# One quarter of u moved inside its own tile, so that 12 of every 84 products read both sides at one place

## The chip, the cores and the metric

The kernel runs on one core of one Trainium2 chip. The metric is the device time of one execution in microseconds (us), the median of several. A core has a matrix engine (TensorE, "PE" in the profile; its weight loads are shown as a row of their own, "PEld"), a vector engine (VectorE, "DVE"), an activation engine (ScalarE, "ACT"), a general engine (GpSimd, "POOL") and a queue engine that issues DMAs (SyncE, "SP").

## The reference

Two layers are computed on a sequence of 512 tokens with 1024 features: a gated recurrent mixer in the first, a dilated attention in the second, and a SwiGLU feed-forward part behind each. The change touches the feed-forward part alone:

```python
def swiglu_ffn(u, w_in, w_out):          # u: 512 x 1024, w_in: 1024 x 5632, w_out: 2816 x 1024
    gate, up = jnp.split(u @ w_in, 2, axis=-1)
    return (jax.nn.silu(gate) * up) @ w_out
```

All of it is float32. The kernel gets there by splitting each operand into a rounded part and a remainder (`hi`, `lo`; type fp32r) and adding three products.

## The kernel before, in words

`u` lies transposed in two tiles, `uh` (the rounded part) and `ul` (the remainder): 128 partitions, 8 slices of features (`kt`), 512 tokens each. Every product of the matrix engine is one of a group of three, issued by `three` on lines 438 to 440: line 438 multiplies hi by hi, line 439 takes the remainder of the side that streams, line 440 the remainder of the weights. In the feed-forward part the weights are loaded into the array (128 columns) and `u` streams through it.

The first few column blocks of `w_in` go by plain products, 512 tokens wide (`block`; 24 products a block). The other 34 blocks, 16 in the first layer and 18 in the second, go by Strassen's scheme in Winograd's form (`seven_products`): a block of 1024 by 256 columns (128 of the gate, 128 of up) is cut into quarters, and so is `u`; seven products of quarters take the place of eight. One product of quarters is one call of `run`: 4 slices of `kt` times `three`, so 12 products on PE, each 256 tokens wide. A block is 7 calls of `run`, 84 products.

The quarters of `u` are slices of `uh` and `ul`: `B11` is slices 0 to 3, tokens 0 to 255; `B21` is slices 4 to 7 of the same tokens; `B22` is slices 4 to 7 of tokens 256 to 511. The fourth quarter, slices 0 to 3 of tokens 256 to 511, isn't a side of a product; it only goes into the sums of quarters. These sums (`t1`, `T3`, `T4`, `t2`) are made once a layer by `token_sums` and lie in tiles of their own, `th` and `tl`. The weights of a block are prepared by DVE, ACT and POOL while PE works on the block before: ACT casts (`r_hi`, line 797; `s_hi`, line 821), DVE subtracts (`r_lo`, line 801; `s_lo`, line 825), and POOL and DVE form sums of quarters (`sum_a` on POOL, line 805; `sum_b`, `sum_c` on DVE, lines 809 and 813). They lie in two sets of tiles in turn, `R` (called `spare` or `hiq`/`loq` in the trace) and `Sm`. The results are put together in `shared` (`sums_1`, `sums_2`, `sums_3`, `finish`, and ACT's copies on lines 884 and 894).

The order of the work inside `seven_products` is written out by hand (`manual_schedule`); what stands ahead of that block is put in order by a scheduler when the program is built.

A word on "place". Each tile begins at a fixed byte of its partition, and place here means that byte modulo 512. In the program as built, `uh` begins at 28288, `ul` at 44672, `th` at 147072 and `tl` at 163456, all at place 128. The weights of `R` and `Sm` begin at 134336, 140480 or 82112, for example, all at place 192, because of an offset of 16 elements (`R0`). In the plain products both sides are at place 128. In the attention layer's `seven_values` the sides are exchanged: slices of `u` and its sums are loaded as weights, at place 128, and the matrix streams, at place 256 (`V0`). Slices of 256 or 512 tokens and of 128 columns are multiples of 512 bytes long, so a tile's place holds for all of its slices.

Of the kernel before, what the change touches and what calls it, by code (L numbers as in the profile page):

```python
# [9 lines left out]
F32 = mybir.dt.float32  # L10
# [148 lines left out]
def block_kernel(tc, x, c, positions, ada_w, ada_b, norm_g, hgrn_w_in, lower, hgrn_norm_g, hgrn_w_out,  # L159
                 attn_w_in, attn_w_out, ffn_w_in, ffn_w_out, inv_freq, out):  # L160
    nc = tc.nc
    act, dve, pool, pe = nc.scalar, nc.vector, nc.gpsimd, nc.tensor
# [5 lines left out]
    with ExitStack() as ctx:  # L168
# [7 lines left out]
        def bank(tag):  # L176
            uid[0] += 1
            return psum.tile([P, 512], F32, name=f"ps_{tag}{uid[0]}", tag=tag, bufs={"mm": 4, "a": 2, "b": 2}[tag])

        def fresh(p, shape, tag, bufs=1, dt=F32):  # L180
            uid[0] += 1
            return p.tile(shape, dt, name=f"{tag}{uid[0]}", tag=tag, bufs=bufs)
# [247 lines left out]
        uh = base.tile([P, KT, S], F32R, name="uh")  # L430
        ul = base.tile([P, KT, S], F32R, name="ul")
# [5 lines left out]
        def three(ps, ah, al, bh, bl, start, stop):  # L437
            pe.matmul(ps, ah, bh, start=start, stop=False)  # L438
            pe.matmul(ps, ah, bl, start=False, stop=False)  # L439
            pe.matmul(ps, al, bh, start=False, stop=stop)  # L440
# [18 lines left out]
        class Turn:  # L459
# [61 lines left out]
            def u_of(self, t, q, ks=range(4)):  # L521
                if ks[0] == 0:
                    self.u[t, q] = fresh(self.pl, [P, 4, P], "u", 4)
                u, b = self.u[t, q], self.b[t][q]
                for k in ks:
                    kt = q * 4 + k
                    A, B, src = self.A[:, kt:kt + 1], self.B[:, kt:kt + 1], b[:, k * P:(k + 1) * P]
                    if q == 0:
                        act.activation(u[:, k], src, AF.Identity, bias=B, scale=A)
                    else:  # L530
                        dve.tensor_scalar(u[:, k], src, A, B, op0=OP.mult, op1=OP.add)
# [239 lines left out]
        def seven_products(fs, mid, sgp, spare, th, tl):  # L771
# [4 lines left out]
            Q4 = lambda a: a.rearrange("p (s n) -> p s n", s=4)  # L776
            u_of = lambda r, c: [(uh[:, r * 4 + k, c * 256:c * 256 + 256], ul[:, r * 4 + k, c * 256:c * 256 + 256]) for k in range(4)]
            t_of = lambda i: [(th[:, i, k], tl[:, i, k]) for k in range(4)]
            B11, B21, B22 = u_of(0, 0), u_of(1, 0), u_of(1, 1)
            t1, T3, T4, t2 = (t_of(i) for i in range(4))  # L780

            W = shared.rearrange("p a (b n) -> p (a b) n", b=2)
# [4 lines left out]
            def places(i):  # L787

                p = i % 2
                if len(ring) <= p:  # L790
                    ring.append((spare if p == 0 else st.part_tiles(R0), st.part_tiles(R0)))
                return ring[p]
# [37 lines left out]
            def run(ps, w, o, us):  # L830
                for kt in range(4):
                    a = slice(o + kt * P, o + (kt + 1) * P)
                    three(ps, w[0][:, a], w[1][:, a], *us[kt], kt == 0, kt == 3)

            def runs(i):
                R, Sm = places(i)
                b = [bank("mm") for _ in range(4)] if i % 2 == 0 else [bank(t) for t in "abab"]
                g_of[i] = b
                half = lambda n, k: b[n][:, k * 256:k * 256 + 256]
                run(half(0, 0), R, 0, B11)  # L840
                run(half(3, 1), R, 512, T4)
                run(half(1, 0), R, 1024, B21)
                run(half(1, 1), Sm, 0, t2)
                run(half(2, 1), Sm, 1024, T3)
                run(half(2, 0), Sm, 512, t1)
                run(half(3, 0), Sm, 1536, B22)
# [20 lines left out]
            with tc.manual_schedule(engines=ORDERED):  # L867
# [9 lines left out]
                for i in range(len(fs)):  # L877
                    more = i + 1 < len(fs)
                    runs(i)
                    sums_3(i - 1)  # L880
                    if more:
                        r_lo(i + 1)
                    finish(i - 1)
                    act.copy(W[:, 2], g_of[i][0][:, 0:256])
                    if more:
                        sum_a(i + 1)
                        sum_b(i + 1)
                        s_hi(i + 1, 0)
                        sum_c(i + 1)
                    sums_1(i)  # L890
                    if more:
                        s_lo(i + 1, 0)
                        s_hi(i + 1, 1)
                    act.copy(W[:, 3], g_of[i][2][:, 0:256])
                    if more:
                        s_lo(i + 1, 1)
                        r_hi(i + 2)
                    sums_2(i)
# [3 lines left out]
        def ffn(l, first, close, nxt, side):  # L902
            turns.close()
            close()
            with ExitStack() as fx:
# [4 lines left out]
                with ExitStack() as qx:  # L910
                    sgp = qx.enter_context(tc.tile_pool(name=f"sg{l}", bufs=1, side=side))
                    qp = qx.enter_context(tc.tile_pool(name=f"quarters{l}", bufs=1, side=bass.opposite_side(side)))
                    spare = [qp.tile([P, 3 * 512 + R0 - k * R0], F32R, name=f"spare{l}{k}")[:, R0 - k * R0:] for k in range(2)]
                    qp.tile([P, 112], F32, name=f"pad_q{l}")
                    th = qp.tile([P, 4, 4, 256], F32R, name=f"th{l}")
                    tl = qp.tile([P, 4, 4, 256], F32R, name=f"tl{l}")
                    for j in range(PLAIN[l]):
                        if j == 0:
                            pss = first
                        else:  # L920
                            pss = []
                            for i in range(2):
                                w = st.take()
                                pss += [block(*w, k * P, 256) for k in range(2)]
                        sg = [fresh(sgp, [P, S], "sg", 2) for _ in range(2)]
                        for k in range(2):
                            act.activation(sg[k], pss[k], AF.Silu)
                        if j == 0:
                            cut = token_sums(th, tl, midt[:, NF - 8:])
                        for k in range(2):  # L930
                            dve.tensor_mul(mid(2 * j + k), pss[2 + k], sg[k])
                        if j == 0:
                            cut()
                            fixed.close()
                    seven_products(range(2 * PLAIN[l], NF), mid, sgp, spare, th, tl)
# [136 lines left out]
        first, vraw, vhi, vlo = {}, {}, {}, {}  # L1072
# [538 lines left out]
        first = mixer_out(oT, otp, (8,), gates.pop((0, 2)), 0, "left", lambda: None)  # L1611
# [263 lines left out]
        first = mixer_out(oT, store[0], (3, 5), gates.pop((1, 2)), 1, "left", cx.close, tail)  # L1875
# [32 lines left out]
```

## Time and profile before

| | us |
|---|---|
| median of 3 runs | 1523.53 (1523.38 to 1524.4) |
| the profiled execution | 1522.98 |
| its span, first instruction to last | 1521.3 |
| PE busy | 1502.2 of the span |
| DVE, ACT, POOL busy | 1062.7, 718.2, 234.1 |
| first stretch of `seven_products` (16 blocks) | from 381.76 to 540.05 |
| second stretch (18 blocks) | from 1216.74 to about 1394.8 |

The profiled execution took 1.7 us more than its span and 0.55 us less than the median. The granted TensorE clock was 0.997 of full speed over the whole span. A row of the timeline gives the start of an instruction in us from the span's start, its length, engine, line, and what it writes and reads; matmuls are pipelined, so the distance from one start to the next is what a product costs, and the length shown is longer.

### The profile page before, as it was taken

The numbers are of one execution on the slowest core, as the hardware profiler recorded it, in microseconds if no ns is written. First come the engines' busy times: TensorE is split into PE (matmuls) and PEld (weight loads), VectorE is DVE, ScalarE is ACT, GpSimd is POOL, SyncE is SP. The second block draws the span as 40 slices with busy tenths as digits, with TensorE's granted clock in tenths as the row PEclk, the third lists the DMA queues.
The fourth block names the chain that finished last, engine by engine and source line by source line (L and its number), as shares of the span: only waits on it lengthen the run. The fifth ranks groups of instructions, "written<-read, shape, count | busy, mean of one in ns | idle before, by whom it ended". The sixth has DMA issues, their size and how long they took to land. (4 is left out here: it accounts for less than half of the span.)

```text
span 1521.3 us, 23536 instructions
## 1 busy us (share of the span) xinstructions
PE 1502.2 (99%) x9231; PEld 1318.0 (87%) x9231; DVE 1062.7 (70%) x1837; ACT 718.2 (47%) x1215; POOL 234.1 (15%) x208
## 2 busy tenths in 40 slices
PE   8999999999999999999999999999999999999998
PEld 6777888898999988888987888988888899999886
DVE  4587867486888896476667766686466978888633
ACT  4443433353444433375546666356655544444231
POOL 1011211031222211140001110011002212221100
PEclk9999999999999999999999999999999999999999
DMA  9554444125333356423166540465222323334521
GB/s 308 183 162 145 149 136 166 56 88 162 112 111 105 103 192 220 163 100 124 56 194 174 146 126 28 129 177 149 73 71 98 111 84 111 112 111 140 199 105 56
DMA packets 206943, 199.14 MB, mean 131 GB/s; under 512 B 6840, under 2 KB 164720, under 8 KB 206576
## 3 DMA queue, kind: packets, MB, share of 16 engines
q1 hardware_dynamic: 203856, 190.87, 40.2%
q10 hardware_dynamic: 1952, 6.65, 1.2%
q8 instruction: 72, 1.18, 0.3%
q0 software_dynamic: 1024, 0.13, 0.2%
q14 instruction: 39, 0.32, 0.1%
HBM read 192.31 MB, written 5.31 MB: 130 GB/s over the span
## 5 line engine op out<-in xcount | busy, mean ns | idle before, releaser
L89 DVE TENSOR_TENSOR lo<-raw,hi 128x2048 fp32r<-128x2048 f32 x68 | 158.8, 2337 | 93.1 <-ACT hi L88 92.9
L88 ACT CAST hi<-raw 128x2048 fp32r<-128x2048 f32 x68 | 129.7, 1908 | 191.6 <-DMA raw<-in_ffn_w_out_dram 53.4
L438 PE MATMUL ps_mm<-apart,hi 128*128 128x512 f32 x384 | 151.4, 394 | 0.0
L439 PE MATMUL ps_mm<-apart,hi 128*128 128x512 f32 x384 | 151.2, 394 | 0.0
L440 PE MATMUL ps_mm<-apart,lo 128*128 128x512 f32 x384 | 150.5, 393 | 0.0
L438 PE MATMUL ps_mm<-uh,hi 128*128 128x512 f32 (+1 forms) x400 | 146.3, 366 | 0.0
L439 PE MATMUL ps_mm<-ul,hi 128*128 128x512 f32 (+1 forms) x400 | 144.3, 361 | 1.0 <-DVE ul L538 1.0
L440 PE MATMUL ps_mm<-uh,lo 128*128 128x512 f32 (+1 forms) x400 | 144.6, 361 | 0.0
L821 ACT CAST hiq<-raw 128x1024 fp32r<-128x1024 f32 x68 | 68.2, 1047 | 66.8 <-DVE raw L809 65.8
L438 PE MATMUL ps_mm<-hi,oh 128*128 128x512 f32 x240 | 94.0, 392 | 0.0
L439 PE MATMUL ps_mm<-lo,oh 128*128 128x512 f32 x240 | 93.4, 389 | 0.0
L438 PEld LDWEIGHTS ps_mm<-uh,hi 128*128 128x128 f32 x400 | 75.5, 189 | 19.7 <-issue 8.4
L439 PEld LDWEIGHTS ps_mm<-ul,hi 128*128 128x128 f32 x400 | 75.6, 189 | 12.1 <-DVE ul L538 1.4
L440 PEld LDWEIGHTS ps_mm<-uh,lo 128*128 128x128 f32 x400 | 75.5, 189 | 11.4
L440 PEld LDWEIGHTS ps_mm<-apart,lo 128*128 128x128 f32 x384 | 72.2, 188 | 14.6 <-DVE lo L89 0.2
L439 PEld LDWEIGHTS ps_mm<-apart,hi 128*128 128x128 f32 x384 | 72.2, 188 | 14.2
L438 PEld LDWEIGHTS ps_mm<-apart,hi 128*128 128x128 f32 x384 | 72.2, 188 | 14.0
L259 DVE SCALAR_TENSOR_TENSOR shared<-raw,cond,shared 128x512 f32<-128x512 f32 x98 | 73.4, 749 | 10.3 <-DMA raw<-in_ada_w_dram 9.2
L825 DVE TENSOR_TENSOR loq<-raw,hiq 128x1024 fp32r<-128x1024 f32 x68 | 80.0, 1219 | 0.4 <-ACT hiq L821 0.4
L261 POOL PARTITION_ALL_REDUCE shared<-shared x14 | 45.9, 3279 | 201.8 <-DVE shared L259 201.8
L805 POOL TENSOR_TENSOR raw<-raw 128x512 f32<-128x512 f32 x34 | 54.6, 1604 | 108.7 <-DVE loq L801 49.3
L809 DVE TENSOR_TENSOR raw<-raw 128x1024 f32<-128x1024 f32 x34 | 41.6, 1225 | 39.1 <-POOL raw L805 39.1
(448 smaller groups left out, 4392.9 us busy)
## 6 DMA issues: line engine op xcount, KB each, us to landing
raw<-in_ada_w_dram SPq DMA_DIRECT2D x40, 1024.0 KB, 5.2
raw<-in_ffn_w_in_dram SPq DMA_DIRECT2D x136, 256.0 KB, 3.6
raw<-in_attn_w_in_dram SPq DMA_DIRECT2D x48, 512.0 KB, 5.2
raw<-in_ffn_w_out_dram SPq DMA_DIRECT2D x22, 1024.0 KB, 5.0
raw<-in_hgrn_w_in_dram SPq DMA_DIRECT2D x12, 1024.0 KB, 5.5
raw<-in_attn_w_in_dram SPq DMA_DIRECT2D x12, 1024.0 KB, 4.9
raw<-in_ffn_w_in_dram SPq DMA_DIRECT2D x10, 1024.0 KB, 5.1
first<-in_ada_w_dram SPq DMA_DIRECT2D x14, 512.0 KB, 7.6
```

Source lines behind the costliest of these rows:

```text
L88: self.nc.scalar.copy(hi, t)
L89: self.nc.vector.tensor_sub(lo, t, hi.bitcast(F32))
L259: dve.scalar_tensor_tensor(a, r[:, k], sc, a, op0=OP.mult, op1=OP.add)
L261: pool.partition_all_reduce(a, a, P, bass.bass_isa.ReduceOp.add)
L438: pe.matmul(ps, ah, bh, start=start, stop=False)
L439: pe.matmul(ps, ah, bl, start=False, stop=False)
L440: pe.matmul(ps, al, bh, start=False, stop=stop)
L805: pool.tensor_add(r[:, 2], r[:, 2], r[:, 0])
L809: dve.tensor_tensor(r[:, 0:2], r[:, 0:3:2], r[:, 1:2].broadcast_to((P, 2, 512)), op=OP.add)
L821: act.copy(hi, src)
L825: dve.tensor_sub(lo, src, hi.bitcast(F32))
```

## The change

`B11` is copied inside `uh` and `ul` from tokens 0 to 255 to elements 144 to 399 of the same slices. 144 elements are 576 bytes, so it then begins at place 192, as the weights do. The target overlaps the source, so the copy is made in two pieces, the upper one first; ACT copies `uh`, DVE copies `ul`, once in each of the two layers. What is overwritten belongs to the fourth quarter, which nothing reads any more. The 12 products of `run(half(0, 0), R, 0, B11)`, the first of each block, now read both sides at place 192; the other 72 are as before, 128 against 192. In block 0 of each layer the first three calls change order, `T4`, `B21`, `B11`. Below the edit every line number is larger by 5.

```diff
-            B11, B21, B22 = u_of(0, 0), u_of(1, 0), u_of(1, 1)
+            B21, B22 = u_of(1, 0), u_of(1, 1)
+
+            for copy, t in ((act.copy, uh), (dve.tensor_copy, ul)):
+                for a, b in ((112, 256), (0, 112)):
+                    copy(t[:, 0:4, a + 144:b + 144], t[:, 0:4, a:b].bitcast(F32))
+            B11 = [(uh[:, k, 144:400], ul[:, k, 144:400]) for k in range(4)]
...
-                run(half(0, 0), R, 0, B11)
-                run(half(3, 1), R, 512, T4)
-                run(half(1, 0), R, 1024, B21)
+                first = [(half(0, 0), R, 0, B11), (half(3, 1), R, 512, T4), (half(1, 0), R, 1024, B21)]
+                for k in (1, 2, 0) if i == 0 else range(3):
+                    run(*first[k])
```

The order of the built program shows where the scheduler put the copies. On PE, at the first layer's step from the plain products to block 0, this stood before (`ps_mm` with a number is an output bank, `spare` the weights of `R`):

```order
L440 MATMUL ps_mm_3313<-uh,lo_3167 128x512
L438 MATMUL ps_mm_3367<-uh,spare_3056 128x256
L439 MATMUL ps_mm_3367<-ul,spare_3056 128x256
L440 MATMUL ps_mm_3367<-uh,spare_3057 128x256
L438 MATMUL ps_mm_3367<-uh,spare_3056 128x256
```

and this stands there now:

```order
L440 MATMUL ps_mm_3313<-uh,lo_3167 128x512
L438 MATMUL ps_mm_3374<-th_3059,spare_3056 128x256
L439 MATMUL ps_mm_3374<-tl_3060,spare_3056 128x256
L440 MATMUL ps_mm_3374<-th_3059,spare_3057 128x256
L438 MATMUL ps_mm_3374<-th_3059,spare_3056 128x256
```

The 12 products of `B11` moved behind the 24 of `T4` and `B21`, and the product of line 438 that begins them waits for ACT's second copy, that of line 439 for DVE's second copy. On DVE the same place read, before:

```order
L931 TENSOR_TENSOR mid_3049<-ps_mm_3288,sg_3338 128x512
L801 TENSOR_TENSOR loq_3363<-raw_3233,hiq_3362 128x1536
L809 TENSOR_TENSOR raw_3233<-raw_3233 128x1024
L931 TENSOR_TENSOR mid_3049<-ps_mm_3313,sg_3339 128x512
L813 TENSOR_TENSOR raw_3233<-raw_3233 128x512
```

and now, with the two copies between `r_lo` and `sum_b` of block 1:

```order
L936 TENSOR_TENSOR mid_3049<-ps_mm_3288,sg_3338 128x512
L806 TENSOR_TENSOR loq_3367<-raw_3233,hiq_3366 128x1536
L783 CAST ul<-ul 128x4x144
L783 CAST ul<-ul 128x4x112
L814 TENSOR_TENSOR raw_3233<-raw_3233 128x1024
L936 TENSOR_TENSOR mid_3049<-ps_mm_3313,sg_3339 128x512
L818 TENSOR_TENSOR raw_3233<-raw_3233 128x512
```

The first of them waits for PE's product of slice 3 of the last plain block, the second for the first. On ACT the copies of `uh` stand behind `r_hi` of block 1 and ahead of the copy out of block 0's first bank (line 884 before, 889 now). POOL and SP issue what they issued, in the same order.

## The prediction

> **What bounds the kernel now.** I read the page first, then the sums of the two stretches of `seven_products`, then PE's timeline at both ends of one, and then the neighbours on DVE, ACT and POOL where the copies go.
>
> ```profile
> PE 1502.2 (99%) x9231; PEld 1318.0 (87%) x9231; DVE 1062.7 (70%) x1837; ACT 718.2 (47%) x1215; POOL 234.1 (15%) x208
> 381.76:540.00 158.24, 158.24 (x1345) 1.00 0.39 114
> ```
>
> The first row is the page's, the second PE's busy time in the first stretch: PE never pauses there (158.24 of 158.24 us, clock 1.00). So only two things can move the time: the distance between products, and a wait that PE doesn't have now. The distance is read from the ends of the stretch:
>
> ```profile
> 381.53 0.39 PE L440 MATMUL ps_mm<-uh,lo 128*128 128x512 f32 x1
> 381.76 0.28 PE L438 MATMUL ps_mm<-uh,spare 128*128 128x256 f32 x1
> 381.88 0.28 PE L439 MATMUL ps_mm<-ul,spare 128*128 128x256 f32 x1
> ...
> 539.93 0.28 PE L440 MATMUL ps_b<-uh,loq 128*128 128x256 f32 x1
> 540.05 0.40 PE L438 MATMUL ps_mm<-hi,oh 128*128 128x512 f32 x1
> ```
>
> 16 blocks of 84 are 1344 products in 540.05 - 381.76 = 158.29 us: 117.78 ns each, from the first product on, for the places 128 against 192. The same width with both sides at one place (128 and 128) stands in the plain part, where 256-wide products run too:
>
> ```profile
> 311.84 0.28 PE L438 MATMUL ps_mm<-uh,hi 128*128 128x256 f32 x1
> 312.07 0.28 PE L440 MATMUL ps_mm<-uh,lo 128*128 128x256 f32 x1
> ...
> 332.81 0.28 PE L438 MATMUL ps_mm<-uh,hi 128*128 128x256 f32 x1
> 337.97 0.28 PE L439 MATMUL ps_mm<-ul,hi 128*128 128x256 f32 x1
> ```
>
> From 332.81 to 337.97 are 43 products: 120.0 ns each. The first pair, which follows 512-wide products, took 0.23 us for two, 115 ns each, before the distance settled. The place thus shifts the distance by 2.22 ns. And one pair of places can have more than one distance: in `seven_values`, 256 against 128, the same kind of product ran
>
> ```profile
> 734.81 0.28 PE L440 MATMUL ps_mm<-hiq,apart 128*128 128x256 f32 x1
> 754.01 0.28 PE L438 MATMUL ps_mm<-hiq,apart 128*128 128x256 f32 x1
> ...
> 957.96 0.28 PE L439 MATMUL ps_a<-loq,uh 128*128 128x256 f32 x1
> 989.76 0.28 PE L439 MATMUL ps_mm<-loq,uh 128*128 128x256 f32 x1
> ```
>
> 160 products in 19.20 us (120.0 ns) in one stretch and 268 in 31.80 us (118.7 ns) in another. There the distance depends on how the run was entered, and holds until a pause.
>
> [...]
>
> **The change part by part.** *The 12 products of B11.* 34 blocks of 12 are 408 products. At the nearest row (both sides at one place) they go from 117.78 to 120.0 ns: 408 x 2.22 ns = +0.91 us. Stepping into and out of this distance may gain or lose something: the pair at 311.84 came 10 ns early at the printed resolution, so I allow 0.01 us x 34 = 0.3 us either way and take nothing.
>
> *The other 72.* 34 x 72 = 2448 products, nothing in them is edited. I take 117.78 ns again, hence 0: the run at 381.76 came straight from 512-wide products at one place and had this distance from its first product on, so it needs no particular start. The ends, by rows: 120.0 ns (+2.22 x 2448 = +5.4 us) and the 115 ns of the pair at 311.84 (-2.78 x 2448 = -6.8 us).
>
> *The copies on ACT* (2 in each layer). Nearest row for the size:
>
> ```profile
> L534 ACT CAST uh<-u x24: 608/619/627, 305.7 to 1182.4; 128x512 fp32r<-128x512 f32 x24
> 379.78 1.47 ACT L797 CAST hiq<-raw 128x1536 fp32r<-128x1536 f32 x1
> 383.37 0.37 ACT L884 COPY shared<-ps_mm 128x256 f32<-128x256 f32 x1 [2.12 <-PE ps_mm L440]
> 1208.51 1.47 ACT L797 CAST hiq<-raw 128x1536 fp32r<-128x1536 f32 x1
> ```
>
> 576 and 448 elements at 619 ns for 512 are 0.70 + 0.54 us, from 381.25 to 382.5, inside the 2.12 us in which ACT was idle. B11 is due behind 24 products, at 381.76 + 24 x 0.1178 = 384.58. Cost 0, with 2.1 us to spare. The copy on line 884 moves too, because its bank is now finished third: 24 products later, 383.37 + 2.83 = 386.2. Its next neighbour on ACT began at 386.25, so that casts for block 1 shift by 0.3 us at most; block 1 begins at 391.65 (84 x 0.1178 later) and asks for these casts after another 36 products, so nothing waits.
>
> *The copies on DVE, first layer.* These are tight.
>
> ```profile
> L1666 DVE CAST apart<-ul x8: 597/613/615, 681.2 to 684.9; 128x512 fp32r<-128x512 f32 x8
> 381.84 1.75 DVE L801 TENSOR_TENSOR loq<-raw,hiq 128x1536 fp32r<-128x1536 f32 x1
> 384.99 1.22 DVE L809 TENSOR_TENSOR raw<-raw 128x1024 f32<-128x1024 f32 x1 [1.40 <-POOL raw L805]
> 383.67 1.29 POOL L805 TENSOR_TENSOR raw<-raw 128x512 f32<-128x512 f32 x1 [7.08 <-DVE loq L801]
> ```
>
> They start when line 801 ends, 383.59. At 613 ns for 512 they take 0.69 + 0.54 us and end at 384.82; the second product of B11 (line 439) is due at 384.70. So PE waits 0.1 us at least. But POOL's `sum_a` starts at 383.67, between them, and POOL and DVE hinder each other:
>
> ```profile
> 15.81 1.27 POOL L1191 TENSOR_TENSOR lo<-raw,hi 128x512 fp32r<-128x512 f32 x1
> 15.88 1.76 DVE L1130 TENSOR_SCALAR late<-h,rr 128x1024 f32<-128x1024 f32 x1
> L1130 DVE TENSOR_SCALAR late<-h,rr x4: 753/754/1757, 7.4 to 15.9; 128x1024 f32<-128x1024 f32 x4
> ```
>
> A one-input DVE instruction of 0.754 us took 1.76 us, ending when POOL's 1.27 us were over and its own time had followed. If POOL gets in between the two copies, the second is held for 1.29 us: at 613 ns for 512 it ends at 383.59 + 0.69 + 1.29 + 0.54 = 386.11 and PE waits 1.4 us; at the 754 ns for 1024 of the held instruction (0.42 and 0.33 us) it ends at 385.63 and PE waits 0.93. I take 0.93, because that instruction is nearest in kind (one input, both sides in SBUF), with 0.1 and 1.4 as ends. `sum_b` (line 809) then starts up to 1.1 us later than 384.99; what it feeds is due at 395.9, after 36 products of block 1, and was ready at about 390.6, so this hides.
>
> [...]
>
> *The copies in the second layer.*
>
> ```profile
> 1216.74 0.28 PE L438 MATMUL ps_mm<-uh,spare 128*128 128x256 f32 x1
> 1214.00 1.23 DVE L809 TENSOR_TENSOR raw<-raw 128x1024 f32<-128x1024 f32 x1 [0.80 <-POOL raw L805]
> 1216.94 0.69 DVE L931 TENSOR_TENSOR mid<-ps_mm,sg 128x512 f32<-128x512 f32 x1 [0.99 <-PE ps_mm L440]
> ```
>
> They wait for slice 3 of the last plain block, 12 wide products (2.7 us) ahead of 1216.74, so they start near 1214.0 and are done by 1215.3; B11 is due at 1219.57. Behind them lines 809 and 813 end at about 1217.2 instead of 1215.95, and line 931 follows 0.3 us late, with 5 us of idle time behind it. Cost 0.
>
> **Sum.** 0.91 + 0.93 = +1.84 us on 1522.98 gives 1524.8 for the profiled execution; on the median, which stands 0.55 us higher, 1525.4. Its own range: 1525.4 - 0.8 - 0.3 = 1524.3 to 1525.4 + 0.5 + 0.3 = 1526.2. A measurement of this kernel tells 0.2%, 3.05 us, from no change.
>
> **The rivals.** *Faster: the 12 products set a better distance for the 72 behind them.* For it: `seven_values` has 120.0 and 118.7 ns at the same places, by entry alone, and the 72 are now entered afresh in each block. Against it: 117.78 was there from the first product at 381.76 and is already below both. A step like that of `seven_values`, 1.33 ns, gives -3.3 us: 1522.1, not to be told from no change. At the 115 ns of 311.84 it gives -6.8: 1518.6. It counts as faster from (3.05 + 1.84) us / 2448 = 2.0 ns on, so at 115.8 ns or less.
>
> *Slower: the 72 fall into 120.0 ns*, held there by the 12, as the stretch at 734.81 was: +5.4 us, 1530.8. For it: 120.0 is the commonest distance of 256-wide products outside this stage. Against it: the entry at 381.76 followed products at one place and didn't do it. It decides from (3.05 - 1.84) / 2448 = 0.5 ns on, above 118.3 ns.
>
> *The place does nothing, and the change not what it says:* 117.78 and 120.0 would differ for another reason, and the 12 stay at 117.78. Then only the wait is left: 1523.53 + 0.93 = 1524.5. [...]
>
> **How the numbers follow.** Forecast 0.46 (of it 0.02 over 1526.58, since steps in and out can cost more), faster rival 0.26 (of it 0.22 below 1520.48), slower rival 0.20, no effect of place 0.08. Faster by over 0.2%: 0.22. Slower: 0.20 + 0.02 = 0.22. Within: 0.44 + 0.04 + 0.08 = 0.56. The likeliest case gives 1525.4. For 8 in 10 the range takes in the slower rival's 1530.8 and the faster one's 1518.6 with 1.6 us below it for a distance somewhat under 115 ns: 1517.0 to 1531.0.
>
> **What would show it.** PE's rows in any block but the first: 12 starts 120 ns apart (1.44 us from the first B11 product to the first of T4), then 72 at 117.78 (8.48 us); a block of 9.92 us instead of 9.89. In the first layer's block 0, a gap on PE behind the first B11 product, put down to DVE, of 0.1 to 1.4 us, and POOL's line 810 or the second copy stretched. In the second layer no gap. The prediction is wrong if the 72 aren't at 117.78, or if a later block shows a wait.

## The result, and the profile after

The changed kernel took 1513.9 us (median of four runs, 1512.73 to 1517.4) against 1523.97 us (1523.38 to 1525.71) for the kernel before beside it: a ratio of 0.9936 with a 95% interval of 0.9916 to 0.9956. It is 10 us faster, where 1525.4 us and no measurable change were forecast. 1513.9 us also lies below the forecast's range, 1517.0 to 1531.0 us. The profiled execution took 1512.75 us. Two later executions, 5312.43 us of the changed kernel and 4799.02 us of the kernel before, were slow ones and enter none of the ratios and ranges given here.

The page's row of engines, and PE's busy time in the first stretch of `seven_products` and in the second (columns: from and to in us, their length, busy time and starts or instructions still running, granted clock, DMA share, GB/s):

```profile
PE 1492.8 (99%) x9231; PEld 1308.2 (87%) x9231; DVE 1063.6 (70%) x1841; ACT 720.3 (48%) x1219; POOL 234.4 (16%) x208
```

```profile
381.63:535.30 153.67, 153.67 (x1345) 1.00 0.40 117
391.35:400.95 9.60, 9.60 (x86) 1.00 0.39 111
1211.69:1384.60 172.91, 172.91 (x1513) 1.00 0.38 111
```

As before, PE never pauses in either stretch, and the clock is 1.00 in both. But 1345 instructions now fit in 153.67 us, where they took 158.24. All the work is still there; the products have moved closer together. The middle row is block 1 alone: 9.60 us, against 9.89 us before. Its rows show where the time went (PE's timeline; the distance between two starts is what a product costs):

```profile
391.35 0.28 PE L438 MATMUL ps_a<-uh,hiq 128*128 128x256 f32 x1
391.47 0.27 PE L439 MATMUL ps_a<-ul,hiq 128*128 128x256 f32 x1
...
392.65 0.28 PE L440 MATMUL ps_a<-uh,loq 128*128 128x256 f32 x1
392.77 0.29 PE L438 MATMUL ps_b<-th,hiq 128*128 128x256 f32 x1
...
394.15 0.28 PE L438 MATMUL ps_b<-uh,hiq 128*128 128x256 f32 x1
...
400.95 0.28 PE L438 MATMUL ps_mm<-uh,spare 128*128 128x256 f32 x1
```

The 12 products of B11, the ones at one place, take 392.77 - 391.35 = 1.42 us. The next 12 take 1.38 us. The remaining 60 take 400.95 - 394.15 = 6.80 us, 113.33 ns each. Before, 60 such products took 7.07 us. The gain lies in the products that the edit doesn't touch. Taken from PE's starts, block 0 of each layer lasts 9.72 us and each of the other 32 blocks 9.60: 2 x 9.72 + 32 x 9.60 = 326.64 us, against 34 x 9.893 = 336.37 before. These 9.73 us are nearly all of the 10.3 us by which the span shrank (1521.3 to 1511.0).

The copies, and the first product of B11 in block 0:

```profile
379.67 1.26 ACT L783 CAST uh<-uh 128x576 fp32r<-128x576 f32 x2
380.36 1.75 DVE L806 TENSOR_TENSOR loq<-raw,hiq 128x1536 fp32r<-128x1536 f32 x1
382.02 1.85 DVE L783 CAST ul<-ul 128x576 fp32r<-128x576 f32 x2
382.18 1.44 POOL L810 TENSOR_TENSOR raw<-raw 128x512 f32<-128x512 f32 x1 [7.09 <-DVE loq L806]
384.46 0.28 PE L438 MATMUL ps_mm<-uh,spare 128*128 128x256 f32 x1
384.58 0.28 PE L439 MATMUL ps_mm<-ul,spare 128*128 128x256 f32 x1
```

DVE's two copies end at 383.87, before the product at 384.58 that needs them, and PE waits for nothing.

### The profile page after: what moved, and what is told of

Same layout as the page of the kernel before. It is cut to its first block, busy times and chain, and to the rows that moved or that the text cites. A ratio compares the mean times of both kernels' runs of the same rounds, so it can differ in the third digit from the quotient of the medians.

```text
span 1511.0 us, 23542 instructions
## 1 busy us (share of the span) xinstructions
PE 1492.8 (99%) x9231; PEld 1308.2 (87%) x9231; DVE 1063.6 (70%) x1841; ACT 720.3 (48%) x1219; POOL 234.4 (16%) x208
## 3 DMA queue, kind: packets, MB, share of 16 engines
q0 software_dynamic: 1024, 0.13, 0.2%
## 5 line engine op out<-in xcount | busy, mean ns | idle before, releaser
L440 PE MATMUL ps_mm<-hi,ol 128*128 128x512 f32 x176 | 68.5, 389 | 0.0
```

## The experiments

The question is what made the other 72 products faster. Four ideas were tried: that the 12 products set an order between the stream and the weight loads which outlasts them (A; B, if it has to be set again in each block); that the copies or the new order of calls did it (C); that any change of place does it; and that 113.33 and 117.78 ns are two steady orders of the same reads, of which PE falls into one by its timing (P). Narrower forms (A1, A2) are stated in the expectations where they are tried.

In each row of windows below, the count holds the starts in the window and one to three products that were still running at its beginning.

### The copies and the order of calls alone

```diff
-                for a, b in ((112, 256), (0, 112)):
-                    copy(t[:, 0:4, a + 144:b + 144], t[:, 0:4, a:b].bitcast(F32))
-            B11 = [(uh[:, k, 144:400], ul[:, k, 144:400]) for k in range(4)]
+                for a, b in ((128, 256), (0, 128)):
+                    copy(t[:, 0:4, a + 128:b + 128], t[:, 0:4, a:b].bitcast(F32))
+            B11 = [(uh[:, k, 128:384], ul[:, k, 128:384]) for k in range(4)]
```

> The changed kernel with the copies moved by 128 elements (512 bytes) in place of 144: the same number of copies, the same order of the calls in block 0, but B11 stays at place 128, 128 against 192 as all others. Theory A and B (place is the cause): all blocks 84 x 117.78 = 9.89 us, time about that of the kernel before, 1523 to 1525 us. Rival C (the copies or the order of the first three calls of block 0 bring the gain): blocks of 9.52 to 9.60 us, about 1514 us.

Measured: 1524.33 us, ratio 0.9993 (0.9978 to 1.0008). Block 1 in its windows:

```profile
391.57:401.46 9.89, 9.89 (x86) 1.00 0.37 108
```

In the profiled execution every block lasted 9.89 us. C falls. Three of the ten runs, at 1517.5 to 1519.2 us, were faster than all 29 of the kernel before beside them. None of the three was profiled, so their cause stays open (see the pause below).

### All 84 products at one place

```diff
-R0, V0 = 16, 32
+R0, V0 = 0, 32
...
-                    qp.tile([P, 112], F32, name=f"pad_q{l}")
+                    qp.tile([P, 128], F32, name=f"pad_q{l}")
```

> The kernel before with R0 = 0: every weight tile of the seven products at place 128, so that all 84 products of a block have both sides at one place; no copies. By the prediction's price of one place (120.0 ns, from the attention layer): 84 x 120.0 = 10.08 us a block, 34 x 0.187 = 6.3 us more, about 1530 us. If place alone does nothing: 1523.5 us.

Measured: 1530.28 us, ratio 1.0038 (1.0026 to 1.0051), and in block 1:

```profile
391.65:401.73 10.08, 10.08 (x86) 1.00 0.37 106
```

10.08 us for 84 products are 120.0 ns, the prediction's price of one place to the digit; in all it came to 6.0 us, against 6.3 expected.

### One place by moving the weights, once a layer

Made from the kernel before. The spare tiles leave room so that, in block 0, the weights that meet B11 lie at place 128, as `u` does. `r_lo` is split in the same way as `r_hi`; `hs` and `ls` are the two spare tiles.

```diff
+            seed, rest = (hs[:, 0:512], ls[:, 1152 - R0:]), (hs[:, 512 + R0:], ls[:, 0:1024])
...
-                    act.copy(places(i)[0][0][:, 0:1536], raw[i][:, 512:])
+                    if i == 0:
+                        act.copy(seed[0], raw[i][:, 512:1024])
+                        act.copy(rest[0], raw[i][:, 1024:])
+                    else:
+                        act.copy(places(i)[0][0][:, 0:1536], raw[i][:, 512:])
...
+                if i == 0:
+                    run(half(0, 0), seed, 0, B11)
+                    run(half(3, 1), rest, 0, T4)
+                    run(half(1, 0), rest, 512, B21)
```

> Made from the kernel before, with no copy of u. In block 0 of each layer the weights of the quarter that meets B11 are written to place 128 (a split of the casts of r_hi and r_lo), so that only the 12 first products of block 0 have both sides at one place (128 against 128); all other products, B11's in the later blocks too, are 128 against 192. Theory A (the 12 products set an order between the stream and the weight loads that lasts until PE stops): the first 12 take about 1.42 to 1.44 us, every later product 113.33 ns, so a block behind the first takes 84 x 113.33 = 9.52 us, 0.08 us less than in the changed kernel, and the time is 1513.9 - 33 x 0.08 = about 1511.2 us. Theory B (the order wears off and has to be set again in each block, or comes from the place of B11 in itself): blocks behind the first go back to 9.89 us, time about 1523.5 us.

Measured: 1524.35 us, ratio 1.0000 (0.9991 to 1.0009). Blocks 0 and 1:

```profile
383.00:392.90 9.90, 9.90 (x85) 1.00 0.32 94
392.90:402.80 9.90, 9.90 (x87) 1.00 0.38 108
```

The 12 did run at one place and came close to 120 ns (they took 1.43 us by PE's starts, 119.2 ns each), and behind them everything went back to 117.78. Theory A fell in this form, and B was not shown either: this kernel steps the weights from place to place, where the changed kernel steps the stream, and its 12 come straight behind 512-wide products. The kernels below that step the weights in every even block, and the stream once a layer, take these two apart.

The same kernel with the weights at place 256, 32 elements behind the stream (`R0, V0 = 32, 32`):

> As the kernel that seeds once, but with the weights 32 elements (128 bytes) behind the stream in place of 16: place 256 against 128. [...] Rival (another distance gives back what the seed brought): 117.8 ns or more, 1523 us and above.

Measured: 1526.66 us, ratio 1.0014 (1.0005 to 1.0023). Block 1:

```profile
391.31:401.29 9.98, 9.98 (x87) 1.00 0.38 107
```

By PE's starts this block takes 9.97 us, 118.7 ns a product, as `seven_values` had before at 256 against 128. What more distance does in the shorter order (113.33 ns) is not shown by this: the run above went back to 117.78 ns behind its 12, so this way of stepping doesn't lead to that order. In the order that it does lead to, more distance took more time and not less (118.7 ns against 117.78).

### The same step of the weights in every even block

```diff
-                    if i == 0:
+                    if i % 2 == 0:
```

> As the kernel that seeds once by its weights, but in every even block (0, 2, 4, ...): there the weights of the 12 first products lie at place 128, the stream stays at 128 everywhere. In blocks 2, 4, ... these 12 come behind 256-wide products at 117.78 ns and not behind 512-wide ones. Theory A1 (only a step of the stream's place sets the order): 12 at 120.0 ns, all else 117.78, about 17 x 0.03 = 0.5 us slower than the kernel before. Theory A2 (what was wrong with the seed-once kernel is that its 12 came behind 512-wide products): blocks from the second on at 113.33 ns, about 1512 us.

Measured: 1524.22 us, ratio 0.9997 (0.9987 to 1.0006). Block 2, which has the 12 at one place behind 256-wide products:

```profile
403.27:413.19 9.92, 9.92 (x87) 1.00 0.36 107
```

9.92 us is 12 x 120 ns and 72 x 117.78. This is exactly the block that the prediction drew. It was right about this step of the weights and wrong about the change's step of the stream. What the 12 come behind makes no difference here, so A2 falls. One difference is left between the two steps: the 12 share place 128 here and place 192 in the changed kernel. Whether the side that moves matters, or the place that both shared, no run here separates.

### One place by moving the stream, once a layer

The changed kernel, with B11 put back to place 128 after block 0:

```diff
                     act.copy(W[:, 2], g_of[i][0][:, 0:256])
+                    if i == 0:
+                        for t in (uh, ul):
+                            for a, b in ((288, 400), (176, 288), (144, 176)):
+                                act.copy(t[:, 0:4, a + 112:b + 112], t[:, 0:4, a:b].bitcast(F32))
...
-                first = [(half(0, 0), R, 0, B11), (half(3, 1), R, 512, T4), (half(1, 0), R, 1024, B21)]
+                first = [(half(0, 0), R, 0, B11 if i == 0 else u_of(0, 1)), (half(3, 1), R, 512, T4), (half(1, 0), R, 1024, B21)]
```

> The changed kernel with B11 copied once more by ACT, after its 12 products of block 0, from place 192 to tokens 256 to 511 of the same slices, which is place 128 again. So only block 0 of each layer has the 12 products at one place (192 against 192), reached by moving the stream; all later blocks are 128 against 192 throughout. Theory A1 (the step of the stream from one place back to 128 sets the order, and it lasts): 113.33 ns in all blocks behind block 0's first three calls, 9.52 us a block, about 1511 us if the added copies hide. Theory B (the order must be set again in each block): later blocks fall back to 9.89 us, about 1523 us.

Measured: 1514.95 us, ratio 0.9937 (0.9923 to 0.9950). Blocks 1, 15 and 33 (the last of each layer), and what PE waited for in the last two:

```profile
391.36:400.88 9.52, 9.52 (x87) 1.00 0.38 112
524.64:534.74 10.10, 9.81 (x87) 1.00 0.40 134
1375.59:1386.47 10.88, 9.79 (x86) 1.00 0.50 178
```

```profile
PE ps_a L440 <- DVE loq L830: 0.3, 1, 0.3
...
PE ps_b L440 <- DVE loq L830: 1.1, 1, 1.1
```

A1 holds: set once, 113.33 ns (9.52 / 84) stays through fourteen blocks without another product at one place, up to the layer's last block. B falls. The expected 1511 us did not come. At 9.52 us a block PE overtakes the preparation of the weights: it waits for DVE's `loq` in the last block of each layer, and these blocks take 0.58 and 1.36 us more than 9.52. That is most of the 32 x 0.08 = 2.6 us that dropping the later steps saves (32 blocks, as the two blocks 0 keep theirs). The trace also has 678.8 us between the last block of layer one and the first of layer two, 2.5 more than the changed kernel's 676.3. This stretch varies from trace to trace, between 676.2 and 678.1 us in kernels whose blocks never ran at 113.33 ns, so most of those 2.5 us say nothing on the step.

### A step of the stream to another place

```diff
-                for a, b in ((112, 256), (0, 112)):
-                    copy(t[:, 0:4, a + 144:b + 144], t[:, 0:4, a:b].bitcast(F32))
+                for a, b in ((96, 256), (0, 96)):
+                    copy(t[:, 0:4, a + 160:b + 160], t[:, 0:4, a:b].bitcast(F32))
-            B11 = [(uh[:, k, 144:400], ul[:, k, 144:400]) for k in range(4)]
+            B11 = [(uh[:, k, 160:416], ul[:, k, 160:416]) for k in range(4)]
```

> The changed kernel with the copies moved by 160 elements: B11 at place 256, so its 12 products read 256 against 192, and never both sides at one place; all else 128 against 192. Theory A1 in its narrow form (it needs one place): no 113.33 ns, 117.8 to 120 ns, 1523 to 1526 us. In its wide form (any step of the stream's place can set the order): 113.33 ns for the 72, about 1512 to 1516 us.

Measured: 1522.87 us, ratio 0.9988 (0.9979 to 0.9998). Block 1:

```profile
391.59:401.49 9.90, 9.90 (x87) 1.00 0.37 108
```

The 12 took 1.417 us and the next 12 1.410, and nothing changed behind them. Not any step does it; of the two tried, the one from 192 against 192 did and the one from 256 against 192 did not.

### A pause in place of a step

The kernel before, with PE made to wait between B11 and T4 in each block:

```diff
                 run(half(0, 0), R, 0, B11)
+                dve.scalar_tensor_tensor(th[:, 2, 0, 0:1], half(0, 0)[:, 0:1], 0.0, th[:, 2, 0, 0:1].bitcast(F32), op0=OP.mult, op1=OP.add)
```

> The kernel before, with no step of any place, but with a wait of PE in each block: between the first call (B11) and the second (T4) DVE rewrites one column of T4 with its own value (zero times a result of B11's bank plus the value), so PE pauses there for a time that depends on DVE. Theory P (113.33 and 117.78 ns are two steady orders of the same reads, and the one that PE falls into depends on the moment at which it starts): after some of the 34 pauses 113.33 ns to the next pause, after others 117.78. Rival (117.78 is the only order without a step of place): 117.78 ns after all pauses. The time is longer by the pauses, 34 times some 0.1 to 2 us.

Measured: 1535.02 us in one run; the pauses cost more than they bring. One of them on PE, and then 60 products behind the pause of block 1 and 60 behind that of block 2:

```profile
395.00 0.28 PE L440 MATMUL ps_a<-uh,loq 128*128 128x256 f32 x1
395.53 0.38 PE L438 MATMUL ps_b<-th,hiq 128*128 128x256 f32 x1 [0.25 <-DVE th L841]
395.75 0.28 PE L439 MATMUL ps_b<-tl,hiq 128*128 128x256 f32 x1
```

```profile
397.05:404.11 7.06, 7.06 (x62) 1.00 0.21 60
407.41:414.22 6.81, 6.81 (x63) 1.00 0.27 81
```

The same places, the same code, no step: 117.7 ns in one block and 113.5 in the next by these rows. By PE's starts, 23 of the 34 blocks ran at 113.33 behind their pause and 11 at 117.78, and each kept its distance until the next pause. So the first half of P is shown: the same reads have two steady orders, at 113.33 and at 117.78 ns.

For the second half, that the timing decides, the same trace speaks. From the last product of B11 to the second product behind the pause it was 746 or 747 ns four times, and 113.33 followed; 748 or 749 ns eight times, and 117.78 followed; 750 to 755 ns 18 times, and 113.33 followed. In the other four, 757 ns (twice) and 815 ns came ahead of 117.78, and 817 ns ahead of 113.33. No length led to both, and behind either order both came. This is one execution, read after it ran, and the start of the second product may already be part of the order that follows: the distance to the first product alone (526 and 527 ns led to both) doesn't tell. So the timing as the cause is likely and not proven.

A nanosecond or two of a pause isn't set by hand, so by a pause it is left to chance, while the step of the changed kernel gave 113.33 in all 34 blocks, in two profiled executions. A chance pause could also explain the three runs of 1517.5 to 1519.2 us with copies at place 128: one layer at 113.33 would give 16 or 18 x 0.37 = 6.0 or 6.7 us, an estimate from the blocks' times. That was not shown.

### Six and three products at one place

```diff
-                    copy(t[:, 0:4, a + 144:b + 144], t[:, 0:4, a:b].bitcast(F32))
-            B11 = [(uh[:, k, 144:400], ul[:, k, 144:400]) for k in range(4)]
+                    copy(t[:, 2:4, a + 144:b + 144], t[:, 2:4, a:b].bitcast(F32))
+            B11 = u_of(0, 0)[:2] + [(uh[:, k, 144:400], ul[:, k, 144:400]) for k in (2, 3)]
```

> The changed kernel with two of B11's four slices (kt 2 and 3) moved and not four, so that 6 products of each block have both sides at one place and not 12, right ahead of the next call. Theory A1 (the order is set where the stream steps back from one place): if 6 are enough to reach it, 113.33 ns for the rest, about 1513 us or a little less; if the order at one place takes longer to settle (in the changed kernel the starts are 117 to 121 ns apart through eight products and 120 from the ninth on), the 72 stay at 117.78 and the time is about 1524 us.

The same with one slice, `u_of(0, 0)[:3]` and `kt` 3:

> The changed kernel with one of B11's four slices (kt 3) moved: 3 products of each block at one place, right ahead of the next call; the copies shrink to a quarter. If three are enough to set the order anew or to leave it as it is: blocks behind the first of 9.52 to 9.56 us, the shorter order from block 0 on, about 1512 us. If the order is reached only from products that have come close to 120 ns apart (six came to 119 and 120 in their last places), block 0 stays at 117.78 ns and so does all behind it: 9.89 us a block, about 1524 us. If it is left by the step of three and not found again, the same.

Measured: 1512.37 us, ratio 0.9928 (0.9909 to 0.9947), for six; 1511.5 us, ratio 0.9916 (0.9903 to 0.9930), for three. Block 1 of each, in this order:

```profile
391.42:400.97 9.55, 9.55 (x86) 1.00 0.39 112
```

```profile
393.72:403.26 9.54, 9.54 (x87) 1.00 0.39 112
```

Both are enough; the distance need not have settled at 120 ns first. Each step costs less as it gets shorter (blocks of 9.60, 9.56 and 9.54 us by PE's starts, with 12, 6 and 3), and PE catches up with DVE in neither. By the blocks' sums, 324.7 us for three against 326.6 for twelve, the version with three products is the best of those run, 1.9 us ahead of the change. The intervals of the two ratios overlap. The changed kernel again, beside the version with six:

> The changed kernel again, beside the others on one chip. Its four runs lay between 1512.7 and 1517.4 us, wider than the 2.3 us of the kernel before. Theory P (the order that PE falls into after a wait depends on the moment): the runs differ by whether other stretches fall into the longer or the shorter order; 1512.5 to 1518 us, and the 34 blocks at 9.60 us again in the trace.

Measured: ratio 0.9940 (0.9924 to 0.9957), runs at 1513.8, 1516.1 and 1516.3 us, and blocks of 9.60 us again. The profiled run was the fastest; why the others are 2 us longer was not seen.

### The same distance for the 512-wide products

```diff
-    def places(self, i, first=0):
+    def places(self, i, first=16):
```

The changed kernel with every hi and lo tile that takes a matrix from the stream begun 16 elements later, at place 192 in place of 128. The 3648 products of 512 tokens took 226.67 ns with both sides at one place (PE's starts between 560 and 640 us in the trace before); here they are 128 against 192, or 192 against 128 where the matrix streams. If they gained what the 256-wide ones did, 120.0 - 117.78 = 2.22 ns or 120.0 - 113.33 = 6.67 ns, they would take 224.4 or 220.0 ns, about 8 or 24 us less in all (an estimate from these distances).

> [...] Rival (the 512-wide products take 226.67 ns at any distance, or PE has to wait for the weights' preparation before it gains): about 1514 us.

Measured: 1520.5 us, ratio 0.9978 (0.9969 to 0.9987), about 6 us longer than the changed kernel. The matrix streaming behind block 15 (492 products of 512) in this kernel, and then the same stretch in the changed kernel:

```profile
541.34 0.39 PE L438 MATMUL ps_mm<-hi,oh 128*128 128x512 f32 x1
653.73 0.40 PE L440 MATMUL ps_a<-hi,ol 128*128 128x512 f32 x1
```

```profile
535.35 0.40 PE L438 MATMUL ps_mm<-hi,oh 128*128 128x512 f32 x1
646.67 0.39 PE L440 MATMUL ps_a<-hi,ol 128*128 128x512 f32 x1
```

112.39 / 491 = 228.9 ns against 226.7; with the matrix as weights, 192 products between 342.83 and 387.39 took 233.3 ns. For the wide products one place is the better choice of these two: neither 224.4 nor 220.0 ns came, nor the rival's 1514 us.

```profile
1221.35 0.28 PE L438 MATMUL ps_mm<-th,spare 128*128 128x256 f32 x1
1224.08 0.28 PE L438 MATMUL ps_mm<-uh,spare 128*128 128x256 f32 x1
```

These two rows of it open its second layer: the 24 products ahead of any at one place took 2.73 us, about 113.7 ns. Its first layer opens with the same 24 behind the same kind of wide products:

```profile
387.62 0.28 PE L438 MATMUL ps_mm<-th,spare 128*128 128x256 f32 x1
390.45 0.28 PE L438 MATMUL ps_mm<-uh,spare 128*128 128x256 f32 x1
```

These took 2.83 us, the longer order (117.8 ns by PE's starts). So wide products at 128 against 192 led once to the shorter order and once to the longer one: another pair of entries where the places alone don't settle it. In the kernel before, entering from wide products at one place gave 117.78 in both layers.

## Why the prediction was wrong

- *The other 72: this step failed.* They were costed at 0 because the run at 381.76 came straight from 512-wide products and had 117.78 ns at once, "so it needs no particular start". That row shows the distance which one entry leads to. It was read as the distance of the places. The places allow two orders, and another start leads to the other (117.78 and 113.33 ns, shown by the pause, and by setting it once). 60 of the 72 went to 113.33 and 12 to 115.0 in each of 32 blocks: 8.18 us instead of 8.48, and in the two blocks 0 about 0.17 us less. That makes the 9.7 us.
- *The faster rival* was this mechanism, with 0.26, but it was sized too small. Its lower end was the 115 ns of a single pair of rows printed to 0.01 us, which gave 1518.6; 113.33 lies below it. The argument against it, that 117.78 was already below both other distances, took the lowest distance seen for a floor.
- *The 12 products of B11.* +0.91 us was forecast, from 120.0 ns. They take 1.42 us, 0.007 more than before, so 0.2 us in 34 blocks: about eight products pass before the distance settles at 120 (in block 1 the starts are 112 to 121 ns apart through eight products and 120 from the ninth on). Their price as such was right (120.0 ns at one place, a 9.92 us block where the weights stepped).
- *The slower rival* (72 at 120.0) did not occur: 120 ended with the last product at one place.
- *That place does nothing* fell: 10.08 us a block at one place.
- *The wait for DVE's copies,* 0.93 us, was 0. The work that prepares block 1 ran 1.48 us earlier than in the trace before (line 806 at 380.36; line 801 had been at 381.84), so the copies began at 382.02 and not at 383.59. The lead goes back to ACT's cast of block 0's weights, which waited for a DMA in both traces, before and after:

```profile
371.94 1.48 ACT L797 CAST spare<-raw 128x1536 fp32r<-128x1536 f32 x1 [5.65 <-DMA raw<-in_ffn_w_in_dram]
370.46 1.48 ACT L802 CAST spare<-raw 128x1536 fp32r<-128x1536 f32 x1 [4.30 <-DMA raw<-in_ffn_w_in_dram]
```

  It was no single chance: in all eight traces of kernels with the copies, line 806 began 0.66 to 2.38 us ahead of block 0's first product, where line 801 began 0.08 us behind it. Why the data came earlier is open. The copies took 1.85 us, 0.62 more than the 1.23 of the bare sum at 613 ns for 512, and 1.10 more than the 0.75 at 754 ns for 1024, with POOL's `sum_a` beside them (1.44 us, 1.29 before). By either, that is less than the 1.29 us of a full hold, and the row at 15.88 that the hold was read from fell short of one too: it ended 17.64, where 17.08 and its own 0.754 us give 17.83. From 383.59 on, 1.85 us would have ended at 385.44, 0.74 us behind the product due at 384.70 (an estimate from these rows), so the wait was sized about right and a start that the prediction didn't question took it away.
- *ACT's copies and those of the second layer* cost nothing, as forecast (1.26 us against 1.24 for ACT's).

## What to carry to other kernels

Products of one width, 256, held steady distances of 113.33, 117.78, 118.7 and 120.0 ns in this case, so such a distance is not a property of the shapes alone. Ask whether the same products show another steady distance anywhere, above all behind a pause, and take a run that was entered in one way as one sample. Where two orders exist, find a cheap step that leads to the better one, set it as rarely and as briefly as it holds, and look for the engine that falls behind once PE speeds up.

## What was unexpected of the hardware

- The same 256-wide fp32r products at 128 against 192 run steadily at 117.78 ns (for whole layers of 16 and 18 blocks) or at 113.33 ns (for 14 and 16 blocks in a row without another step). No steady stretch of 256-wide products here came below 113.33 ns.
- Stepping the stream away from a shared place 192 set the shorter order (113.33 ns); stepping the weights away from a shared place 128, with the same 128 against 192 behind it and the same count of products, did not (117.78 ns). Which of the two differences decides is open, and so is why the place matters to the distance at all: only PE's starts were seen.
- At one place the 256-wide products are at their slowest steady distance (120.0 ns; at other distances 113.33 to 120.0), and the 512-wide ones at the best seen (226.7, against 228.9 and 233.3).
